# Two gates of the third branch among the mixers' last steps, two LoRA inputs projected later, and block values turned in written order

## The chip, the cores and the metric

The kernel runs on one core of a Trainium2 chip. The metric is the device time of one execution in microseconds (us), inputs and outputs in the chip's memory. A core has five engines that run side by side and are joined by semaphores: TensorE (PE) for matmuls, VectorE (DVE), ScalarE (ACT), GpSimd (POOL) and SyncE (SP), which here issues the DMA transfers of the weights.

## The reference

One layer of an encoder trunk, 256 positions, model width 2048, all in float32. After a norm, one projection feeds three branches: stick-breaking attention (4 heads of 128), forgetting attention (4 heads of 128) and an RWKV-7 time mixer (16 heads of 64), each weighted by a gate of its own:

```
u = rms_norm(x)
sb, fox, rw, gates = split(u @ w_in)
y_a = stick_breaking_attention(sb)
y_b = forgetting_attention(fox)            # with a forget logit per head
y_c = rwkv7_time_mix(rw)                   # r, k, v and LoRA inputs of decay, iclr and gate
g_a, g_b, g_c = split(sigmoid(gates))
m = g_a * (y_a @ P_a) + g_b * (y_b @ P_b) + g_c * (y_c @ P_c)
x = x + rms_norm(m @ w_out)
x = x + rms_norm(relu(rms_norm(x) @ w_up)**2 @ w_down)
```

Inside the time mixer each position is mixed with the one before it (a shift with weights mu), the decay comes from `tanh(wd) @ w_up`, the output gate from `sigmoid(gd) @ g_up`; a state per head runs through four chunks of 64 positions, and the output is normed per head.

## The kernel before

**Precision and weights.** Every large product is made of three float32r products: a value x is split into a high part (`hi`, a copy on ScalarE, L144) and a rest (`lo`, a subtraction on VectorE, L145), and hi*hi, hi*lo and lo*hi are summed in PSUM. All weights lie in one stream `wst` of tiles of 128 x 1024 (512 KB) in the order of use. `wraw` loads the next (L136, on SP's queue, three buffers `raw`), `wsplit` makes `whi` and `wlo` from it (three buffers each), and `wnext` keeps one split tile ahead. The stages are, in order: q and k of the first branch; its v; three LoRA inputs `zx` (decay and iclr), `zy` and `zz` (gate; `zz` also holds the forget logits); q, k, v of the second branch; k, r, v of RWKV heads 0 to 7 and then 8 to 15; gates and branch products of the first two branches; those of the third; W_out; the MLP.

**Two kinds of big product.** `unit` makes 128 features for all positions (L160, L164, L166; 16 tiles of `upk`, the split normed input). `tok` makes 512 features for the two halves of the positions (two PSUM tiles; L204, and L189 for its last tiles): for each pair of 128-row blocks of weights 8 matmuls with `whi` and 4 with `wlo`, all of 512 columns. `gate` is a `tok` over `upk` with a tanh into `th`; `branch` is a `tok` over a branch's split outputs (`ya`, `yb`, `ycp`), whose result is multiplied by the gate and added to the block's value `m` (L809 to L812). There are four blocks of 512 features.

**The mixers.** The recurrences and attentions themselves are small matmuls with much work on VectorE and ScalarE between. They are written as generators (`sb_mix`, `fox_mix`, `rwkv_lora`, `rwkv_half(0)` and `rwkv_half(1)`) that yield after each step. `tick` is called by `unit` and `tok` every few matmuls: it adds 0.62 of its argument to a credit and takes steps as long as there is credit. A yield `("stage", cost, hold)` also stops the steps until `hold` ticks have passed (2 by default). That is how small matmuls come to stand between big ones, on TensorE in the order in which they are written: `tc.manual_schedule` keeps TensorE to that order, while the other engines' order is chosen by the scheduler. `order.__exit__` ends this, and behind it the scheduler sets TensorE's order too.

**The steps of an RWKV half** that the prediction speaks of, with the lines of the profile: a triangular solve in 31 small steps on VectorE (L618, L620), transposes of its result (L624, L628), products of 32 x 32 blocks (L633, L640), and then for each of four chunks c: the right-hand side (L659 from c = 1, L663, copied to `rh` by L667), the solve (L672, copied to `Xt` by L676 and L678), and state and output (L683 from c = 1, L689, L692; the state `Pb` is updated by L698 and L700, the output copied by L702). Then the output norm for two pairs of heads each: squares L714, sums L718, gate products L721 and L724, rsqrt, and the products that finish `y` (L731 to L734), which becomes `yc[p]`.

**Where the third branch stands.** Behind the four blocks of the first two branches, a loop takes all steps that are left (`while not fin[0]: step()`), `order.__exit__` follows, the eight `yc` are split to `ycp`, and each block g does: gate, branch product, then four turns of the block's value: two transposes to PSUM (L835) and a split into `pk`, the operand of W_out. The pool `pk` has 24 buffers: 16 hold `upk` until the last gate, 8 hold `ycp`.

Of the kernel before, what the change touches and what calls it, by code (L numbers as in the profile page):

```python
# [49 lines left out]
def hybrid_block(ctx, tc, xt, x, gains, params, consts, lora, gup, wst, out):  # L50
# [47 lines left out]
    hold = [0.0]  # L98

    def step():  # L100

        if mix[0] is None or fin[0] or (wait[0] is not None and wait[0] not in done):
            return False
        wait[0] = None
        try:
            r = next(mix[0])
        except StopIteration:
            fin[0] = True
            return False
        if isinstance(r, tuple):  # L110
            if r[0] == "need":
                wait[0] = r[1]
                return True
            credit[0] -= r[1]
            if r[0] == "stage":
                hold[0] = r[2] if len(r) > 2 else 2.0
            return r[0] != "stage"
        credit[0] -= r
        return True

    def tick(f=1.0):

        credit[0] = min(credit[0] + f * SHARE, 1.5)
        hold[0] -= f
        while hold[0] <= 0 and credit[0] > 0 and step():
            pass


    wpos = [0]

    wq = []
    side = []

    def wraw(n=None):
        raw = wpool.tile([128, HALF], F32, tag="raw", name=nm("raw"), bufs=3)
        nc.sync.dma_start(out=raw, in_=wst[wpos[0] if n is None else n])  # L136
        if n is None:
            wpos[0] += 1
        return raw
# [232 lines left out]
    def fox_mix():  # L372
# [16 lines left out]
        V.tensor_tensor_scan(lf, one, m0, 0.0, ALU.mult, ALU.add)  # L389
        yield ("stage", 2.0, 6)  # L390
        ps = mps()
# [35 lines left out]
        for h in range(4):  # L427
            V.tensor_scalar(w[:, h, 0:128], w[:, h, 0:128], ri[:, h:h + 1], None, ALU.mult)
            V.tensor_scalar(w[:, h, 128:384], w[:, h, 128:384], ri[:, 4 + h:5 + h], None, ALU.mult)
            yield ("stage" if h == 3 else "go", 0.4, 4)  # L430
        for hp in range(2):
# [42 lines left out]
    def rwkv_half(hf):  # L474
# [160 lines left out]
        for g in range(4):  # L635
            A.activation(TW[32:64, g:32:4, :], ps[32 * g:32 * g + 32, 0:256].rearrange("p (a b) -> p a b", a=8), AF.Copy)
        yield ("stage", 0.2, 3)
        ps = mps()
# [3 lines left out]
        for g in range(4):  # L642
            A.activation(SC[0:32, g:32:4, 32:64], ps[32 * g:32 * g + 32, 0:256].rearrange("p (a b) -> p a b", a=8),
                         AF.Copy)
        yield ("stage", 0.2, 3)

# [5 lines left out]
        for c in range(4):  # L652
# [13 lines left out]
            for hc in HC:  # L666
                A.activation(rhs[:, :, hc], psr[hc, 0:T].rearrange("p (a b) -> p a b", a=4), AF.Copy)  # L667
            yield ("stage", 0.9)
            pso = [mps(), mps()]
# [3 lines left out]
            for i, p in enumerate(PR):  # L673
                for hc in HC:
                    if i < 2:
                        V.tensor_copy(Xt[p][0:64, c, hc], pso[0][hc, co[i]])  # L676
                    else:
                        A.activation(Xt[p][0:64, c, hc], pso[1][hc, co[i]], AF.Copy)  # L678
            yield ("stage", 0.9)
            psy = mps()  # L680
# [20 lines left out]
            for i, p in enumerate(PR):  # L701
                A.activation(y[p][:, c * 64:c * 64 + 64], psy[:, co[i]], AF.Copy)  # L702
            yield ("stage", 2.0)

        for i2 in range(2):
# [7 lines left out]
            for i in range(2):  # L713
                A.activation(sc[:, i, :], y[PR[2 * i2 + i]], AF.Square)  # L714
            yield ("stage", 0.1)
            ps = mps()
# [8 lines left out]
            A.activation(var, ps.rearrange("p (a b) -> p a b", a=2), AF.Identity, scale=1.0 / 64, bias=cst[:, 1:2])  # L725
            yield ("stage", 0.1)
            rsqrt(ri, var, sc)
# [31 lines left out]
    for br in ("sb", "fox"):  # L759
# [10 lines left out]
        done[br + "v"] = vtok()  # L770
        if br == "sb":
            done["sb"] = True
            for i, (nme, n) in enumerate((("zx", 128), ("zy", 128), ("zz", 36))):
                ps = unit(upk)
                z = rp.tile([64 if n == 36 else n, T], F32, name=nme)
                shift(ps, MU_X + i, z[0:n], n)
                done[nme] = z
            done["lora"] = True
        else:
            done["fox"] = True  # L780

# [13 lines left out]

    def gate():
        ths = []
        for ps in tok(upk):
            th = rp.tile([128, 512], F32, tag="th", name=nm("th"), bufs=3)
            A.activation(th, ps, AF.Tanh, scale=0.5)  # L800
# [14 lines left out]
    for g in range(4):  # L815
        m = rp.tile([128, 2, 512], F32, tag="m", name=nm("m"), bufs=4)
        branch(ya, gate(), m, True)
        branch(yb, gate(), m, False)
        ms.append(m)
    while not fin[0]:  # L820
        step()
    order.__exit__(None, None, None)
    ycp = []
    for p in range(8):
        y = pk()
        split(yc[p], y)
        ycp.append(y)
    mpk = []
    for g in range(4):
        thc = gate()  # L830
        branch(ycp, thc, ms[g], False)
        for j in range(4):
            ps = mps()
            for tt in range(2):
                PE.transpose(ps[:, tt * 128:tt * 128 + 128], ms[g][:, tt, j * 128:j * 128 + 128], C("ident"))  # L835
            u = pk()
            split(ps[:, 0:T], u, 0.5)
            mpk.append(u)
    p1.close()
# [24 lines left out]

    g2, loads = gain(0, [fm().rearrange("p a b -> p (a b)")[:, 0:512] for _ in range(4)])
    x1 = [p2.tile([128, D], F32, tag="x1", name=nm("x1"), bufs=2) for _ in range(2)]
# [15 lines left out]
    for g in range(4):  # L882
        gs = slice(512 * g, 512 * g + 512)
        for tt, ps in enumerate(tok(mpk, 4 if g == 3 else 1)):
            def gained():
# [418 lines left out]
```

## Time and profile before

| what | us |
|---|---|
| median of 3 runs | 1560.79 |
| lowest, highest | 1556.21, 1565.39 |
| the profiled execution | 1562.27 |
| its span from first to last instruction | 1560.5 |
| steps of RWKV half 0 up to its first output norm | 361.83 to 440.02 |
| the same steps of half 1, and its second output norm | 592.37 to 643.08 |
| from there to the second set of turns | 643.08 to 667.98 |

A line of the profile names the source line, the engine, what is written and read, the shape, and how many instructions; a line of the timeline begins with start and length in us, and a bracket at its end tells how long the engine was idle before it and who released it. Matmuls are pipelined: one of 512 columns is listed at about 0.39 us, but the next starts earlier, so lengths overlap and starts are what counts. In a table by stretch the columns are the stretch, its length, busy time and number of instructions of TensorE, the mean granted clock (1.00 is full speed), the busy share of the DMA engines, and GB/s.

### The profile page before, as it was taken

How to read it: one execution, taken by the hardware profiler on the slowest of the kernel's cores; microseconds unless marked ns; L12 is line 12 of the kernel's file. 1: busy time of each engine (PE TensorE's matmuls, PEld its weight loads, DVE VectorE, ACT ScalarE, POOL GpSimd, SP SyncE). 2: the span in 40 equal slices, each digit the busy share in tenths (PEclk: the TensorE clock that was granted, in tenths of full speed). 3: DMA queues.
4: the chain of work that ended last, by engine and by line, in shares of the span. 5: the costliest groups of instructions: out<-in, count | busy, mean ns of one | idle time of the engine just before them, and what ended most of it. 6: DMA issues, size and time to landing. Idle time of an engine off the chain costs nothing.

```text
span 1560.5 us, 22381 instructions
## 1 busy us (share of the span) xinstructions
PE 1524.2 (98%) x8318; PEld 1265.7 (81%) x8318; DVE 1157.1 (74%) x1566; ACT 907.9 (58%) x1369; POOL 88.5 (6%) x146
## 2 busy tenths in 40 slices
PE   7999999999999999999999999999999999999997
PEld 6888887887887787788887888888888877888885
DVE  7765568896558896645555778789988899888855
ACT  7565367545466554644444766567766676666542
POOL 0030001100001100000000000000000000000000
PEclk9999999999999998999999999999999999999999
DMA  7645554455445553355695557798888888887764
GB/s 242 206 159 176 162 165 150 138 190 189 135 144 179 174 164 96 125 180 188 228 306 164 171 188 201 216 266 254 242 257 250 230 236 239 263 253 232 214 200 136
DMA packets 101197, 308.50 MB, mean 198 GB/s; under 512 B 10080, under 2 KB 12512, under 8 KB 101088
## 3 DMA queue, kind: packets, MB, share of 16 engines
q1 hardware_dynamic: 91344, 280.66, 55.1%
q0 software_dynamic: 6912, 25.17, 8.7%
q8 instruction: 65, 1.06, 0.3%
q10 hardware_dynamic: 2832, 1.24, 0.3%
q14 instruction: 44, 0.36, 0.1%
HBM read 279.77 MB, written 2.10 MB: 181 GB/s over the span
## 4 chain that ended last, share of the span: by engine, by line
PE 66%; issue 10%; DVE 10%; DMA 9%; ACT 4%; POOL 0%; ACTq 0%; SPq 0%; POOLq 0%; DVEq 0%
PE gps L204 27%; PE gps L160 15%; PE gps L164 8%; DMA raw<-raw 5%; PE gps L189 5%; DVE wlo L145 5%; DMA raw<-in_wst_dram 4%; ACT whi L144 2%; PE gps L166 1%; PE mps L1069 1%; PE mps L1071 1%; PE mps L1070 1%; PE gps L1071 1%; PE gps L1069 1%; PE gps L1070 1%
## 5 line engine op out<-in xcount | busy, mean ns | idle before, releaser
L145 DVE TENSOR_TENSOR wlo<-raw,whi 128x1024 fp32r<-128x1024 f32 x590 | 716.1, 1223 | 272.4 <-ACT whi L144 254.4
L144 ACT ACTIVATE whi<-raw 128x1024 fp32r<-128x1024 f32 x590 | 618.2, 1055 | 342.0 <-PE gps L204 153.8
L160 PE MATMUL gps<-pk,whi 128*128 128x512 f32 x1501 | 386.2, 395 | 2.1 <-ACT whi L144 1.0
L160 PEld LDWEIGHTS gps<-pk,whi 128*128 128x128 f32 x1501 | 278.2, 189 | 62.4 <-issue 5.8
L204 PE MATMUL gps<-whi,pk 128*128 128x512 f32 x1144 | 293.8, 395 | 0.4 <-ACT whi L144 0.4
L204 PEld LDWEIGHTS gps<-whi,pk 128*128 128x128 f32 x1144 | 213.5, 189 | 47.0 <-issue 1.3
L164 PEld LDWEIGHTS gps<-pk,wlo 128*128 128x128 f32 x1608 | 220.1, 191 | 16.0 <-DVE wlo L145 0.7
L164 PE MATMUL gps<-pk,wlo 128*128 128x256 f32 x1608 | 225.9, 283 | 0.1
L204 PE MATMUL gps<-wlo,pk 128*128 128x512 f32 x572 | 159.8, 397 | 0.4 <-DVE wlo L145 0.4
L204 PEld LDWEIGHTS gps<-wlo,pk 128*128 128x128 f32 x572 | 107.3, 190 | 24.2 <-DVE wlo L145 1.1
L991 ACT ACTIVATE tmp<-gps 128x256 f32<-128x256 f32 x64 | 24.6, 384 | 90.7 <-PE gps L166 90.7
L1069 PE MATMUL mps<-whi,fm 128*128 128x512 f32 x192 | 76.1, 396 | 0.8 <-ACT whi L144 0.7
L1071 PE MATMUL mps<-wlo,fm 128*128 128x512 f32 x192 | 75.5, 393 | 0.4 <-DVE wlo L145 0.2
L1070 PE MATMUL mps<-whi,fm 128*128 128x512 f32 x192 | 75.0, 391 | 0.0
L1036 POOL DMA_DIRECT2D raw<-raw x48 | 41.9, 873 | 554.2 <-DVE raw L1033 313.2
L189 PE MATMUL gps<-whi,pk 128*128 128x512 f32 x264 | 71.3, 393 | 0.0
L1071 PE MATMUL gps<-wlo,fm 128*128 128x512 f32 x144 | 57.2, 397 | 2.4 <-DVE wlo L145 2.1
L1033 DVE TENSOR_TENSOR raw<-raw,raw 128x1024 f32<-128x1024 f32 x48 | 58.7, 1223 | 1.0
L189 PEld LDWEIGHTS gps<-whi,pk 128*128 128x128 f32 x264 | 49.2, 188 | 11.2 <-issue 0.7
L1069 PE MATMUL gps<-whi,fm 128*128 128x512 f32 x144 | 56.8, 395 | 1.4 <-ACT whi L144 1.4
L1070 PE MATMUL gps<-whi,fm 128*128 128x512 f32 x144 | 56.5, 392 | 0.0
L204 PE MATMUL gps<-whi,fm 128*128 128x512 f32 x208 | 51.4, 389 | 0.0
(294 smaller groups left out, 1551.7 us busy)
## 6 DMA issues: line engine op xcount, KB each, us to landing
raw<-in_wst_dram SPq DMA_DIRECT2D x518, 512.0 KB, 4.4
raw<-raw POOLq DMA_DIRECT2D x48, 512.0 KB, 6.7
x<-in_x_dram SPq DMA_DIRECT2D x8, 256.0 KB, 6.5
out_dram<-x SPq DMA_DIRECT2D x8, 256.0 KB, 2.8
x<-in_xt_dram SPq DMA_DIRECT2D x3, 512.0 KB, 7.3
fm<-in_gains_dram SPq DMA_DIRECT2D x4, 256.0 KB, 5.5
pk<-in_gains_dram SPq DMA_DIRECT2D x4, 256.0 KB, 4.5
con<-in_consts_dram SPq DMA_DIRECT2D x1, 576.0 KB, 7.8
```

The lines of the kernel that those rows point to most:

```text
L144: A.activation(hi, raw, AF.Copy)
L145: V.tensor_tensor(lo, raw, hi.bitcast(F32), ALU.subtract)
L160: PE.matmul(ps, hi[:, i * 128:i * 128 + 128], pks[i], start=first and i == 0, stop=False)
L164: PE.matmul(ps[:, 0:T], lo[:, i * 128:i * 128 + 128], pks[i][:, 0:T], start=False, stop=False)
L189: PE.matmul(ps[tt], pks[k][:, c:c + 128], w[:, (k - k0) * 512:(k - k0) * 512 + 512], start=k == 0 and part == 0 and w is hl[0], stop=w is ...
L204: PE.matmul(ps[tt], pks[k][:, c:c + 128], w[:, (k - k0) * 512:(k - k0) * 512 + 512], start=k == 0 and part == 0 and w is hl[0], stop=False)
L991: A.activation(b, ps[0][:, T:2 * T], AF.Copy)
L1033: V.tensor_tensor(R[a], R[a], R[b], ALU.add)
L1036: G.dma_start(out=R[a], in_=R[b], accum_op=ALU.add)
L1069: PE.matmul(Q[f], a, w, start=d == 0 and i == 0, stop=False)
L1070: PE.matmul(Q[f], b, w, start=False, stop=False)
L1071: PE.matmul(Q[f], a, wl, start=False, stop=d == 3 and i == 1)
```

## The change

It has five parts, and leaves the arithmetic as it was.

1. The first two gates of the third branch are made before the loop that takes the remaining steps, so under the written order and with ticks (`thc`; the second one's tanh goes to free buffers of the pool `BK`). Weights are still in their old places in the stream, so `wraw` follows a small table of jumps.
2. `order.__exit__` moves behind the third block of W_out: the third branch and most of W_out keep the written order. The turns become hooks: one is taken at each tick, those of blocks 0 to 2 from the 13th tick of the last block's gate on, those of the last block from the fifth tick of W_out on.
3. `yc[p]` is split as soon as it is there, at any tick (`cut`).
4. `zx` and `zy` are projected behind the second branch; `zz` stays where it was.
5. Holds of several steps are shorter (6 to 4, 4 to 3, 3 to 2, 2 to 1, 2 to 1.7), and one has no hold. The gains of the norm behind W_out are loaded at once, and no longer one for each weight tile.

```diff
+    each, hooks = [], []
...
         while hold[0] <= 0 and credit[0] > 0 and step():
             pass
+        for f in each:
+            f()
+        if hooks:
+            hooks.pop(0)()
...
+    gc = wst.shape[0] - 256 - 32 - 48
+    jump = {23: 28, 53: 24, 27: 54, gc + 7: gc + 12, gc + 19: gc + 8, gc + 11: gc + 20}
...
-            wpos[0] += 1
+            wpos[0] = jump.get(wpos[0], wpos[0] + 1)
...
-        yield ("stage", 2.0, 6)
+        yield ("stage", 2.0, 4)
...
-            yield ("stage" if h == 3 else "go", 0.4, 4)
+            yield ("stage" if h == 3 else "go", 0.4, 3)
...
-        yield ("stage", 0.2, 3)
+        yield ("stage", 0.2, 2)
...
-            yield ("stage", 0.9)
+            yield ("stage", 0.9, 1)
...
-            yield ("stage", 2.0)
+            yield ("stage", 1.5, 1.7)
...
-            yield ("stage", 0.1)
+            yield ("stage", 0.1, 1)
...
-            yield ("stage", 0.1)
+            yield ("stage", 0.1, 0)
...
-        if br == "sb":
-            done["sb"] = True
-            for i, (nme, n) in enumerate((("zx", 128), ("zy", 128), ("zz", 36))):
...
+        done[br] = True
+        for i, nme, n in ((0, "zx", 128), (1, "zy", 128)) if br == "fox" else ((2, "zz", 36),):
+            ps = unit(upk)
...
+    ycp = [None] * 8
+
+    def cut():
+        for p in range(8):
+            if yc[p] is not None and ycp[p] is None:
+                ycp[p] = pk()
+                split(yc[p], ycp[p])
+
+    cut()
+    each.append(cut)
+    thc = [gate(), gate("BK", 8)]
     while not fin[0]:
         step()
-    order.__exit__(None, None, None)
...
+    cut()
+    each.clear()
+    mpk = [None] * KT
+
+    def turn(g, j):
+        ps = mps()
+        for tt in range(2):
+            PE.transpose(ps[:, tt * 128:tt * 128 + 128], ms[g][:, tt, j * 128:j * 128 + 128], C("ident"))
+        mpk[4 * g + j] = pk()
+        split(ps[:, 0:T], mpk[4 * g + j], 0.5)
+
     for g in range(4):
-        thc = gate()
-        branch(ycp, thc, ms[g], False)
...
+        if g == 3:
+            hooks.extend([lambda: None] * 12 + [lambda k=k: turn(k // 4, k % 4) for k in range(12)])
+        branch(ycp, thc.pop(0) if thc else gate(), ms[g], False)
+    hooks.extend([lambda: None] * 4 + [lambda j=j: turn(3, j) for j in range(4)])
+    wo = tok(mpk)
+    lead = [next(wo)]
...
-    g2, loads = gain(0, [fm().rearrange("p a b -> p (a b)")[:, 0:512] for _ in range(4)])
+    g2, now = gain(0, [fm().rearrange("p a b -> p (a b)")[:, 0:512] for _ in range(4)])
+    for f in now:
+        f()
+    loads = []
...
-        for tt, ps in enumerate(tok(mpk, 4 if g == 3 else 1)):
+        if g == 3:
+            order.__exit__(None, None, None)
+        for tt, ps in enumerate(itertools.chain(lead, wo) if g == 0 else tok(mpk, 4 if g == 3 else 1)):
```

Lines move by 10 to 12 in the new file: L633 is L643 there, L640 is L650, L663 is L673, L672 is L682, L683 is L693, L724 is L734, L835 is L847, and of the big matmuls L189 and L204 are L199 and L214. The order of instructions on an engine is shown at two places; a row is an instruction, what it writes and reads, its size, and a count.

TensorE before, at the first block products of RWKV half 1 (`SC` and `TW` are its solved blocks, `gps_6078` and `gps_6079` the two PSUM tiles of the third branch's first gate):

```order
L633 MATMUL mps_5664<-TW_5660,SC_4702 32x32 x32
L204 MATMUL gps_6078<-whi_5624,pk_281 128x512 x2
L204 MATMUL gps_6079<-whi_5624,pk_281 128x512
L640 MATMUL mps_5701<-SC_4702,TW_5660 32x32 x2
L204 MATMUL gps_6079<-whi_5624,pk_281 128x512
L204 MATMUL gps_6078<-whi_5624,pk_286 128x512
L640 MATMUL mps_5701<-SC_4702,TW_5660 32x32
L204 MATMUL gps_6078<-whi_5624,pk_286 128x512
L640 MATMUL mps_5701<-SC_4702,TW_5660 32x32 x29
L663 MATMUL mps_5744<-Xt_5287,SC_4702 64x64 x2
```

and TensorE of the change at the same products (`gps_5472` and `gps_5473` belong to the last gate of the second branch here):

```order
L643 MATMUL mps_5510<-TW_5406,SC_4413 32x32 x32
L214 MATMUL gps_5472<-whi_5494,pk_401 128x512 x2
L214 MATMUL gps_5473<-whi_5494,pk_401 128x512 x2
L214 MATMUL gps_5472<-whi_5494,pk_406 128x512 x2
L214 MATMUL gps_5473<-whi_5494,pk_406 128x512 x2
L214 MATMUL gps_5472<-wlo_5495,pk_401 128x512
L214 MATMUL gps_5473<-wlo_5495,pk_401 128x512
L214 MATMUL gps_5472<-wlo_5495,pk_406 128x512
L214 MATMUL gps_5473<-wlo_5495,pk_406 128x512
L214 MATMUL gps_5472<-whi_5549,pk_461 128x512 x2
L214 MATMUL gps_5473<-whi_5549,pk_461 128x512 x2
L650 MATMUL mps_5575<-SC_4413,TW_5406 32x32 x32
```

Before, three big matmuls stand ahead of the second product and single ones in its midst; now sixteen stand between the two products, and the second one is whole. Counted in weight pairs of the stream, the first product stands at the 182nd pair before and at the 174th now; on VectorE the last of the transposes L628 (L638 now) stands behind the 183rd weight split before and behind the 169th now.

TensorE before, at the first turns of a block's value (`m_3359`; `gps_6330` and `gps_6331` belong to the next gate):

```order
L204 MATMUL gps_6330<-whi_6286,pk_281 128x512 x2
L204 MATMUL gps_6331<-whi_6286,pk_281 128x512
L835 MATMUL mps_6306<-ident,m_3359 128x128
L835 MATMUL mps_6312<-ident,m_3359 128x128
L835 MATMUL mps_6318<-ident,m_3359 128x128
L835 MATMUL mps_6324<-ident,m_3359 128x128
L204 MATMUL gps_6331<-whi_6286,pk_281 128x512
```

and TensorE of the change at its first turns, in the last block's gate:

```order
L214 MATMUL gps_6762<-whi_6819,pk_521 128x512 x2
L847 MATMUL mps_6845<-ident,m_3384 128x128 x2
L214 MATMUL gps_6761<-whi_6819,pk_526 128x512 x2
L214 MATMUL gps_6762<-whi_6819,pk_526 128x512 x2
L214 MATMUL gps_6761<-wlo_6820,pk_521 128x512
L214 MATMUL gps_6762<-wlo_6820,pk_521 128x512
L847 MATMUL mps_6857<-ident,m_3384 128x128 x2
```

Before, the first turns stand right behind the block's third-branch product; now they stand three blocks later, both transposes of a turn side by side, with two to six big matmuls between turns.

More of the change, by code (lines that the diff above doesn't have):

```diff
@@ L1 @@
+import itertools
 import math
@@ L644, in rwkv_half @@
                          AF.Copy)
-        yield ("stage", 0.2, 3)
+        yield ("stage", 0.2, 2)
         Pb = rp.tile([128, 4, 128], F32, tag="Pb", name=nm("Pb"), bufs=1)
@@ L678, in rwkv_half @@
                         A.activation(Xt[p][0:64, c, hc], pso[1][hc, co[i]], AF.Copy)
-            yield ("stage", 0.9)
+            yield ("stage", 0.9, 1)
             psy = mps()
@@ L770, in hybrid_block @@
         done[br + "v"] = vtok()
-        if br == "sb":
-            done["sb"] = True
-            for i, (nme, n) in enumerate((("zx", 128), ("zy", 128), ("zz", 36))):
[L774 to L780, printed above, removed]
+        done[br] = True
+        for i, nme, n in ((0, "zx", 128), (1, "zy", 128)) if br == "fox" else ((2, "zz", 36),):
+            ps = unit(upk)
+            z = rp.tile([64 if n == 36 else n, T], F32, name=nme)
+            shift(ps, MU_X + i, z[0:n], n)
+            done[nme] = z
+    done["lora"] = True
     for hf in range(2):
@@ L794, in hybrid_block, with gate @@
     ya, yb = done["ya"], done["yb"]
-    def gate():
+    def gate(tag="th", bufs=3):
         ths = []
         for ps in tok(upk):
-            th = rp.tile([128, 512], F32, tag="th", name=nm("th"), bufs=3)
+            th = rp.tile([128, 512], F32, tag=tag, name=nm("th"), bufs=bufs)
             A.activation(th, ps, AF.Tanh, scale=0.5)
@@ L819, in hybrid_block @@
         ms.append(m)
+    ycp = [None] * 8
[7 more added lines that the diff above has]
+    thc = [gate(), gate("BK", 8)]
     while not fin[0]:
         step()
-    order.__exit__(None, None, None)
[L823 to L828, printed above, removed]
-    for g in range(4):
-        thc = gate()
-        branch(ycp, thc, ms[g], False)
[L832 to L838, printed above, removed]
+    cut()
[7 more added lines that the diff above has]
+        split(ps[:, 0:T], mpk[4 * g + j], 0.5)
+    for g in range(4):
+        if g == 3:
[4 more added lines that the diff above has]
+    lead = [next(wo)]
     p1.close()
```

## The prediction

> **What bounds the kernel now.** I read the page's busy shares first, then the waits of TensorE, then tables by stretch for the stages that the change touches, and last the timeline around each wait.
>
> ```profile
> PE 1524.2 (98%) x8318; PEld 1265.7 (81%) x8318; DVE 1157.1 (74%) x1566; ACT 907.9 (58%) x1369; POOL 88.5 (6%) x146
> PE   7999999999999999999999999999999999999997
> PEclk9999999999999998999999999999999999999999
> ```
>
> TensorE is busy 98% of the span, and the change neither adds nor removes a matmul. So time can only come from three places: waits of TensorE, stretches at a lower clock, and switches that make matmuls slower than their steady pitch. That pitch:
>
> ```profile
> 433.95 1.98 PE L204 MATMUL gps<-whi,pk 128*128 128x512 f32 x8
> 435.76 1.07 PE L204 MATMUL gps<-wlo,pk 128*128 128x512 f32 x4
> 436.67 1.07 PE L204 MATMUL gps<-whi,pk 128*128 128x512 f32 x4
> ```
>
> Twelve matmuls of 512 columns ("big" below; one pair of weight tiles) start between 433.95 and 436.67: 2.72 us, so 0.2267 us each. With this a stage can be weighed. Half 0 of the RWKV steps (from its L633 to the end of its first output norm, L724) runs among big matmuls under the written order. Half 1 does the same in the drain loop, with little beside it. The first three rows below are all of TensorE in half 0, in half 1 and in the stretch behind half 1; the next three are the same windows with big matmuls alone.
>
> ```profile
> 361.83:440.02 78.19, 78.19 (x709) 1.00 0.50 159
> 592.37:643.08 50.71, 47.91 (x545) 0.90 0.30 95
> 643.08:667.98 24.90, 22.44 (x95) 0.93 0.43 135
> 361.83:440.02 78.19, 62.41 (x257) 1.00 0.50 159
> 592.37:643.08 50.71, 25.71 (x81) 0.90 0.30 95
> 643.08:667.98 24.90, 21.52 (x85) 0.93 0.43 135
> ```
>
> Half 0: 78.19 - 257 x 0.2267 = 19.9 us for its small matmuls. Half 1: 50.71 - 81 x 0.2267 = 32.3 us. Its window holds one output norm more (640.52 to 643.08, 2.6 us), so 29.8 us stand against 19.9: **9.9 us too many**. The third stretch: 24.90 - 85 x 0.2267 = 5.6 us for eight turning matmuls (some 0.1 us each), **4.8 us too many**. Together 14.7 us, and the views say what they are:
>
> ```profile
> PE mps L835 <- DVE m L812: 2.1, 1, 2.1
> PE mps L640 <- DVE SC L628: 2.0, 1, 2.0
> PE mps L718 <- ACT gn L714: 0.8, 1, 0.8
> ...
> 593.05 0.97 PE L204 MATMUL gps<-whi,pk 128*128 128x512 f32 x3
> 594.00 1.90 DVE L628 STREAM_TRANSPOSE SC<-Ti 32x1024 f32<-32x1024 f32 x1
> 596.04 0.25 PE L640 MATMUL mps<-SC,TW 32*32 32x32 f32 x4 [2.02 <-DVE SC L628]
> ...
> 598.00:608.00 10.00, 10.00 (x98) 0.50 0.49 159
> ```
>
> Three waits make 4.9 us (columns: total, times, longest). The clock column is a mean, and in half 1 it is 0.90: 10% of 50.71 us, 5.1 us, is lost to a stretch at half clock, which begins within 2 us of the wait for L628; 0.93 of 24.90 us loses 1.7 us more behind the wait for L812. That is 11.7 of 14.7 us. The rest is cutting: L640 and L659 are split by single big matmuls here, and each split costs.
>
> **The change, part by part.** *Two gates under the written order.* Two gates of the third branch are two times eight pairs of weight tiles: 16 x 2.72 = 43.5 us of big matmuls, which no step of half 1 has to wait for. Which engine is late there: L628 turns the solved triangles on VectorE, L640 reads them. Before, the last L628 stands behind the 183rd weight split of VectorE and L640 at the 183rd weight pair of TensorE, so nothing lies between. Now they stand at the 169th and the 176th (L638 and L650 in the new file). VectorE works in order and TensorE cannot pass the 169th pair before the next split, which is behind the transposes: six pairs, 16 us, cover a wait of 2.0. Its half-clock stretch should go with it, and the steps stand whole as in half 0. Term: -9.9 us. Behind the last step TensorE has 68 big matmuls left before the first that reads yc, and 36 more before the one that reads its last pair: 23.6 us, against the 9.4 us of the norm's chain (below) and four products and splits of some 0.4 us behind it. No wait there.
>
> *Turning in written order.* Turns of the first three blocks start twelve ticks into the last gate, those of the last block four ticks into W_out's first block, when block values have long been added. The wait for L812 and its half clock go: -4.8 us. But 32 transposes come in 16 visits where there were 11. Two visits of four in a calm stretch:
>
> ```profile
> 755.00:775.00 20.00, 19.99 (x93) 1.00 0.68 214
> 755.00:775.00 20.00, 19.41 (x85) 1.00 0.68 214
> ```
>
> 85 records (two cut by the window's ends) x 0.2267 and eight transposes leave 0 to 0.4 us, so 0 to 0.2 us a visit; 5 more visits are 0 to 1 us, and if every visit paid the 0.36 us that a split pays, 1.8 us. I take 0.9.
>
> *Shorter holds.* Steps of the recurrence now follow after one tick, in both halves. What each needs when its engines are free is seen in half 1, where nothing else was in the way:
>
> ```profile
> 616.27 0.68 PE L663 MATMUL mps<-Xt,SC 64*64 64x64 f32 x16
> 617.06 0.78 ACT L667 ACTIVATE rh<-mps 64x256 f32<-64x256 f32 x2 [2.52 <-PE mps L663]
> 617.79 0.78 PE L672 MATMUL mps<-rh,SC 64*64 64x64 f32 x16
> 618.38 0.98 DVE L676 COPY Xt<-mps 64x64 f32<-64x64 f32 x4 [1.81 <-PE mps L672]
> 618.61 0.95 ACT L678 ACTIVATE Xt<-mps 64x64 f32<-64x64 f32 x4 [0.77 <-PE mps L672]
> 619.54 0.69 PE L689 MATMUL mps<-Xt,Kt 128*64 128x64 f32 x16
> 620.05 0.64 PE L692 MATMUL mps<-SC,Xt 128*64 128x64 f32 x16
> 620.29 0.88 DVE L698 TENSOR_TENSOR Pb<-mps,Pb 64x256 f32<-64x256 f32 x2 [0.94 <-PE mps L689]
> 621.20 0.87 DVE L700 TENSOR_TENSOR Pb<-Pb,ecol 64x256 f32<-64x256 f32 x2
> 621.75 0.33 PE L659 MATMUL mps<-Pb,Bt 128*64 128x64 f32 x2
> ...
> L145 DVE TENSOR_TENSOR wlo<-raw,whi 128x1024 fp32r<-128x1024 f32 x590 | 716.1, 1223 | 272.4 <-ACT whi L144 254.4
> L144 ACT ACTIVATE whi<-raw 128x1024 fp32r<-128x1024 f32 x590 | 618.2, 1055 | 342.0 <-PE gps L204 153.8
> ```
>
> L663 to L672 takes 1.5 us from start to start, 0.9 behind the end of L663; L672 to L689 is 1.75 us, 1.05 behind its end; L689 to L659 is 2.2 us. The order now leaves at the least 6 big matmuls for the first (1.36 us), 6 to 8 and mostly L683 besides for the second (1.36 to 2.8 us), 12 and L692 for the third (3.4 us). All fit. A weight split of 1.06 us on ScalarE ahead of L667 would make 0.6 us of wait, one of 1.22 us on VectorE ahead of L676 0.9 us where L683 is not between, two ahead of Pb 0.8 us. On ScalarE the order sets a split behind each pair of steps rather than between, so I take 0; the bound is eight first steps x 0.6, two second ones x 0.9 and six third ones x 0.8: 11.4 us over both halves. Below nothing: TensorE was not waiting in half 0 (clock 1.00, no row of waits), so an earlier half 0 gains nothing.
>
> *Second output norm.* It waits for the buffer of the first:
>
> ```profile
> 631.11 0.70 PE L724 MATMUL mps<-zz,gup 32*128 32x256 f32 x4
> 640.07 0.71 ACT L714 ACTIVATE gn<-g 128x256 f32<-128x256 f32 x2
> 640.52 1.13 PE L718 MATMUL mps<-gn,con 128*128 128x256 f32 x4 [0.78 <-ACT gn L714]
> ```
>
> The chain takes 9.4 us; the order now leaves 48 big matmuls, 10.9 us, but two tanh of 0.6 us come in on ScalarE. So the 0.8 us wait may stay or go; the 9.9 us count it as gone, so I add +0.8 to be fair, of 0 to 1.5.
>
> *Inputs of decay and gate later.* Three projections, shifts and their activations change places; TensorE's count, the number of table loads (23) and SP's 543 transfers stay. The stream's jumps are other addresses for the same 512 KB tiles. Three memsets of 0.1 us move on POOL, which is idle. Their first user comes some 300 rows later on TensorE. Term 0. In that stretch the clock drops once, without any wait:
>
> ```profile
> 182.31 1.97 PE L401 MATMUL mps<-foxf,ident 4*128 4x256 f32 x8
> 184.00:190.00 6.00, 6.00 (x26) 0.72 0.22 79
> ```
>
> 0.28 x 6 is 1.7 us; it may fall elsewhere or vanish: -1.7 to +1.7, taken as 0.
>
> *Gain loads at once, splits of yc per tick.* SP issues the gains two weight tiles later, where they wait for the last turn, and weights queue behind them.
>
> ```profile
> raw<-in_wst_dram SPq DMA_DIRECT2D x518, 512.0 KB, 4.4
> ```
>
> The first weight behind them is read 60 big matmuls (13.6 us) after that turn; landing and both splits take 4.4 + 1.06 + 1.22 = 6.7 us. Covered; if not, a wait of the difference, none here. Eight splits of yc are the same instructions, earlier. Term 0.
>
> **Sum.** -9.9 - 4.8 + 0.9 + 0.8 = -13.0 us. The profiled execution took 1562.3 us (span 1560.5), so it would take 1549.3; the median of the runs shown, 1560.8, lies 1.5 lower, so I predict **1547.8 us**.
>
> **The rivals.**
> *The half clock stays (chance 0.07).* It may follow from many small matmuls, not from the waits: at 184 us it fell without a wait. Against it: half 0 has the same small matmuls at 1.00. If both stretches stay, 5.1 + 1.7 us come back: 1554.6. [...]
> *Shorter holds become waits (0.14).* ScalarE and VectorE hold a weight split ahead of a step more often than the order of before suggests. Two thirds of the bound, 7.6 us, comes back: 1555.4. For it: 1.36 us of cover against 0.9 + 1.06. Against: the engines' order.
> *Waits that gate the clock: slower (0.04).* The place is L663 to L672 in both halves. If each step waits as bounded (11.4 us) and the waits, which come every 10 us or so, each bring a half-clock stretch like the one of 1.7 us, eight of these add 13.6 us: 1547.8 + 25 = 1572.8. It decides from about 13 us given back, so from where waits begin to gate; the wait of 0.78 us before L718 did not (598 to 608 alone makes up the mean of 0.90).
> *It does not do what it says:* steps left for a drain behind the gates. The order shows L734, the last step, inside the second gate, so I give this no chance of its own.
>
> **How the numbers follow.** Forecast 0.75, rivals 0.07, 0.14, 0.04. A measurement tells about 0.5% (7.8 us, so 1553 and 1568.6) from no change. The forecast is faster, and a fifth of the second rival's cases too: 0.78. The other cases of the first two are within: 0.18; slower 0.04. The range of eight in ten: low -14.7 - 1.7 and some 3 us of scatter between runs, 1541; high takes in both middle rivals, 1557.
>
> **What would show it.** Right: no row of waits for L640 (now L650) or for L835 (L847); half 1's small matmuls cost about 20 us as half 0's; the granted clock is 1.00 from half 1 to W_out. Wrong: rows that wait for rh, Xt or Pb in both halves; a clock below 0.95 in half 1; a wait before the first matmul that reads the last yc; or whi and wlo as the releasers of big matmuls there.

## The result and the profile after

| | before | changed kernel |
|---|---|---|
| median of 7 runs, us | 1562.17 | 1547.59 |
| lowest, highest | 1556.21, 1565.39 | 1542.72, 1551.39 |
| the profiled execution | 1562.27 | 1549.40 |
| its span | 1560.5 | 1547.6 |

The ratio is 0.9906, with a 95% interval from 0.9885 to 0.9927: 14.6 us faster by the medians, 12.9 by the profiled executions. The page's busy shares and the row of the clock:

```profile
PE 1515.7 (98%) x8318; PEld 1262.7 (82%) x8318; DVE 1155.4 (75%) x1566; ACT 908.4 (59%) x1369; POOL 92.9 (6%) x146
PEclk9999999999999999999999999999999999999998
```

The number of matmuls is the same, and TensorE's share is 98% as before, so the share says nothing about the gain. The waits of TensorE do (columns: total, times, longest); these are all of 0.3 us and more:

```profile
PE gps L170 <- ACT whi L154: 9.0, 2, 8.4
PE mps L931 <- DVE x L900: 2.1, 2, 1.9
PE gps L1095 <- DVE wlo L155: 1.5, 4, 0.6
PE gps L1093 <- ACT whi L154: 1.4, 1, 1.4
PE mps L1095 <- DVE wlo L155: 1.0, 3, 0.5
PE gps L199 <- DVE wlo L155: 0.9, 1, 0.9
PE gps L170 <- DVE tmp L1016: 0.8, 3, 0.3
PE gps L174 <- DVE wlo L155: 0.8, 1, 0.8
PE mps L931 <- DVE pk L236: 0.7, 1, 0.7
PE mps L1093 <- ACT whi L154: 0.7, 1, 0.7
PE gps L214 <- DVE wlo L155: 0.3, 1, 0.3
PE mps L650 <- ACT TW L646: 0.3, 2, 0.2
```

The three rows of before that carried 4.9 us (L640 for the solve, L835 for a block's value, L718 for the second output norm) have no successor: L650 now waits 0.3 us, and for ScalarE; L847 and L728 have no row. Next, half 1 in a table by stretch, from its first product L643 to the end of its second output norm: all of TensorE, then big matmuls alone.

```profile
571.45:644.03 72.58, 72.58 (x685) 1.00 0.42 139
571.45:644.03 72.58, 54.51 (x221) 1.00 0.42 139
```

72.58 - 221 x 0.2267 = 22.5 us for small matmuls. Without the second norm (641.58 to 644.03, 2.45 us) that is 20.0 us, where 29.8 stood before and half 0 had 19.9. The clock is 1.00.

**One stretch for all kernels.** To compare kernels whose steps stand in different places, I count big matmuls in TensorE's order. From the 2400th to the 3200th lie, in each kernel below, all of half 1 from L643 on and all 32 turning matmuls, and nothing else besides the 800 big ones; 1297 records of TensorE each time (one straddles the edge). Its length is "the stretch" from here on. Before, then after:

```profile
563.26:786.66 223.40, 218.13 (x1297) 0.97 0.53 169
```

```profile
564.10:772.00 207.90, 207.90 (x1297) 1.00 0.55 181
```

The stretch is 15.5 us shorter. The 1000 big matmuls ahead of it, which hold half 0, went the other way by 1.6 us, the rest of the program by 1.0: -15.5 + 1.6 + 1.0 = -12.9, the difference of the two profiled executions.

### The profile page after: what moved, and what is told of

Same layout as the page of the kernel before. It is cut to its first block, busy times and chain, and to the rows that moved or that the text cites. A ratio compares the mean times of both kernels' runs of the same rounds, so it can differ in the third digit from the quotient of the medians.

```text
span 1547.6 us, 22370 instructions
## 1 busy us (share of the span) xinstructions
PE 1515.7 (98%) x8318; PEld 1262.7 (82%) x8318; DVE 1155.4 (75%) x1566; ACT 908.4 (59%) x1369; POOL 92.9 (6%) x146
## 4 chain that ended last, share of the span: by engine, by line
PE 74%; DVE 9%; issue 8%; DMA 6%; ACT 2%; POOL 0%; SPq 0%; DVEq 0%; POOLq 0%; ACTq 0%
PE gps L214 29%; PE gps L170 15%; PE gps L174 9%; PE gps L199 7%; DVE wlo L155 4%; DMA raw<-raw 4%; DMA raw<-in_wst_dram 3%; PE mps L1093 1%; PE mps L1095 1%; ACT whi L154 1%; PE mps L1094 1%; PE gps L1095 1%; PE gps L176 1%; PE gps L1093 1%; PE gps L1094 1%
## 5 line engine op out<-in xcount | busy, mean ns | idle before, releaser
L214 PE MATMUL gps<-whi,pk 128*128 128x512 f32 x1144 | 291.7, 394 | 0.0
L214 PEld LDWEIGHTS gps<-whi,pk 128*128 128x128 f32 x1144 | 212.0, 188 | 46.0 <-issue 2.3
L214 PE MATMUL gps<-wlo,pk 128*128 128x512 f32 x572 | 155.3, 391 | 0.3 <-DVE wlo L155 0.3
L214 PEld LDWEIGHTS gps<-wlo,pk 128*128 128x128 f32 x572 | 106.8, 188 | 23.0 <-DVE wlo L155 0.8
L199 PE MATMUL gps<-whi,pk 128*128 128x512 f32 x264 | 72.0, 395 | 0.0
L199 PEld LDWEIGHTS gps<-whi,pk 128*128 128x128 f32 x264 | 48.7, 188 | 10.8 <-issue 0.5
L214 PE MATMUL gps<-whi,fm 128*128 128x512 f32 x208 | 51.4, 389 | 0.0
```

Of the source, the lines that this page charges most:

```text
L199: PE.matmul(ps[tt], pks[k][:, c:c + 128], w[:, (k - k0) * 512:(k - k0) * 512 + 512], start=k == 0 and part == 0 and w is hl[0], stop=w is ...
L214: PE.matmul(ps[tt], pks[k][:, c:c + 128], w[:, (k - k0) * 512:(k - k0) * 512 + 512], start=k == 0 and part == 0 and w is hl[0], stop=False)
```

## The experiments

Each kernel was timed in five rounds beside the kernel before on the same chip, except the probe. "The drain" is the loop that takes the steps which are left. Line numbers are those of each kernel's own file; they differ from the changed kernel's by a few. In the edits, `...` stands for lines left out, and the table of jumps, which follows the places of gates and inputs, is adapted in each kernel and mostly not shown. Most single removals come first, then parts alone, then a probe of the clock. The table puts the results together. Its second column is half 1's first product, its third the place of the drain (both in big matmuls of TensorE's order), and the stretch is that of one profiled execution each. The medians come from four sets of rounds, in which the kernel before took 1560.9 to 1562.2 us; the ratios compare within a set.

| kernel | half 1 from | drain at | stretch, us | median, us | ratio, 95% interval |
|---|---|---|---|---|---|
| before | 2529 | 2529 | 223.4 | | 1 |
| gates alone | 2613 | 2721 | 221.7 | 1558.93 | 0.9987 (0.9972 to 1.0003) |
| holds, second mixer and half 0 | 2485 | 2529 | 216.5 | 1554.73 | 0.9961 (0.9945 to 0.9977) |
| holds alone | 2485 | 2529 | 214.6 | 1553.28 | 0.9953 (0.9937 to 0.9970) |
| holds and inputs | 2433 | 2529 | 212.4 | 1551.63 | 0.9937 (0.9915 to 0.9959) |
| gates and holds | 2485 | 2721 | 214.2 | 1553.81 | 0.9947 (0.9926 to 0.9969) |
| changed | 2433 | 2721 | 207.9 | 1547.59 | 0.9906 (0.9885 to 0.9927) |
| changed, old turns | 2433 | 2721 | 208.9 | 1547.20 | 0.9911 (0.9892 to 0.9931) |
| changed, old inputs | 2485 | 2721 | 209.6 | 1546.72 | 0.9910 (0.9893 to 0.9927) |
| changed, one gate | 2433 | 2625 | 219.1 | 1555.76 | 0.9969 (0.9947 to 0.9992) |
| changed, gates undone | 2433 | 2529 | 224.7 | 1562.88 | 1.0016 (1.0002 to 1.0030) |
| changed, old holds | 2565 | 2721 | 224.9 | 1560.97 | 1.0003 (0.9991 to 1.0015) |
| four gates, old holds, old turns | 2565 | 2913 | 211.6 | 1547.61 | 0.9931 (0.9904 to 0.9958) |

### The gates undone

```diff
-    thc = [gate(), gate("BK", 8)]
+    thc = []
```

and the table of jumps without the gates' entries.

> The changed kernel with the two gates of the third branch back behind the drain; everything else of the change stays. Theory (the gates' big matmuls cover half 1's steps): the stretch from half 1's first step to the end of its norms is 10.9 us shorter in the changed kernel than in the one before at the same work, and this comes back nearly whole: 8 to 12 us, so 1556 to 1560 us; a row of waits for L650 on the triangle transposes of about 2 us, and a clock below 0.95 in half 1. Rival (shorter holds and an earlier start of half 1 make the gain, the gates only stand nearby): under 3 us come back, so below 1551, and no wait for L650.

1562.88 us, 15.3 above the changed kernel's median. Waits of TensorE:

```profile
PE mps L728 <- ACT gn L724: 7.9, 2, 6.9
PE mps L669 <- DVE Pb L710: 1.5, 1, 1.5
PE mps L682 <- ACT rh L677: 0.5, 1, 0.5
PE mps L650 <- ACT TW L646: 0.2, 1, 0.2
```

The stretch:

```profile
563.84:788.49 224.65, 214.51 (x1297) 0.95 0.49 167
```

The loss is larger than expected and sits elsewhere: not at L650, since half 1 starts early enough for its solve, but in the last steps and norms. Since the order is written out up to W_out here, the drain stands bare: nothing lies between its steps, and each chain is waited for in full, the norm's with 6.9 us. In the kernel before, the scheduler put big matmuls of the first gate between them, one to four at a time, and 34 between the two norms. So this removal also shows what part 2 does to a drain, and not the gates alone. The clock is 0.50 from 611.56 to 632.03 us, right through that drain.

### Turning as before

```diff
-        if g == 3:
-            hooks.extend([lambda: None] * 12 + [lambda k=k: turn(k // 4, k % 4) for k in range(12)])
         branch(ycp, thc.pop(0) if thc else gate(), ms[g], False)
-    hooks.extend([lambda: None] * 4 + [lambda j=j: turn(3, j) for j in range(4)])
+        for j in range(4):
+            turn(g, j)
```

with the order released behind the drain.

> The changed kernel with the merged blocks turned behind each gate and product, outside the written order, as before; the two gates stay ahead. Theory (TensorE waits for the last addition of a block because the turns follow it at once): a wait of about 2 us for the first turn and a half-clock stretch behind it come back, 4.6 us in all, so 1552 us (1551 to 1554). Rival (that wait came from the drain, whose late yc made the first block late): with the gates ahead there is no wait for L847 either way, and under 1.5 us come back.

1547.20 us, and this theory falls: no wait for the turns, the clock 1.00, and a stretch 1.0 us longer than the changed kernel's.

```profile
563.63:772.52 208.89, 208.88 (x1297) 1.00 0.53 181
```

### The old holds

```diff
-            yield ("stage", 0.9, 1)
+            yield ("stage", 0.9)
...
-            yield ("stage", 1.5, 1.7)
+            yield ("stage", 2.0)
```

and the others as in the diff of the change, all in reverse.

> The changed kernel with the longer holds of before between the steps, in both halves. Theory (the shorter holds cost the 1.6 us that half 0 lost, and half 1 has room for the longer ones inside the two gates): half 0 gets 1 to 1.6 us back, the row of waits for L650 on ScalarE goes, and half 1 stays: 1546 to 1548 us. Rival (without the shorter holds half 1's last steps fall behind the gates): the last steps stand in a drain again and lose 2 to 5 us there, so 1549 to 1552.

1560.97 us: the whole gain is gone, and both expectations were far too small. Half 1 starts at the 2565th big matmul instead of the 2433rd, only its first two rounds fit ahead of the drain at 2721, and the rest stands bare as above:

```profile
PE mps L728 <- ACT gn L724: 7.9, 2, 6.9
PE mps L669 <- DVE Pb L710: 1.2, 1, 1.2
```

### The inputs where they were

```diff
-        for i, nme, n in ((0, "zx", 128), (1, "zy", 128)) if br == "fox" else ((2, "zz", 36),):
+        for i, nme, n in ((0, "zx", 128), (1, "zy", 128), (2, "zz", 36)) if br == "sb" else ():
```

> The changed kernel with the inputs of decay and gate projected where they were before. Theory (their place is worth nothing to TensorE): within 1 us of the changed kernel, 1547 to 1548.5; the one half-clock stretch near 170 us may move. Rival (the later place delays the mixers' early steps, or half 1 starts early only because of it): half 1's steps move by several weight pairs and 2 us or more are lost or won.

1546.72 us, as the theory has it, although half 1 starts 52 big matmuls later: all of it still ends ahead of the drain. The stretch is 1.7 us longer, which the medians don't show.

### Two parts alone: gates and holds

The kernel before with parts 1, 3 and the holds of part 5; behind the drain it goes on as before.

```diff
+    cut()
+    each.append(cut)
+    thc = [gate(), gate("BK", 8)]
     while not fin[0]:
         step()
+    cut()
+    each.clear()
     order.__exit__(None, None, None)
```

> The kernel before with two parts of the change alone: the two gates (with the splits of yc per tick) and the shorter holds. Turning, the inputs of decay and gate, and the gain loads stay as before. Theory (the whole gain is that no step of half 1 is left to the drain, which takes both parts together): the full gain, 1546 to 1549 us, no wait for L640's or L835's successors, clock 1.00 from half 1 to W_out. Rival (the written turns or the other parts carry some of it, hidden in the single removals): 1550 to 1554.

1553.81 us: half of the gain, inside the rival's range. One wait is back, for the first turn (L848 here):

```profile
PE mps L848 <- DVE m L819: 2.1, 1, 2.1
```

```profile
562.49:776.70 214.21, 211.27 (x1297) 0.99 0.53 179
```

So the wait ahead of the first turn is no part of half 1. Two kernels differ from this one in little, and neither has it: with the inputs later (and the gains at once) it is "changed, old turns", 5.3 us shorter in the stretch; with turns in written order (and the gains at once) it is "changed, old inputs", 4.6 us shorter. In the first, half 1's last norm stands 54 big matmuls earlier, and VectorE is through with it when the first block is finished; in the second nobody reads the block at once. Either cover is enough, which is why removing one of the two cost next to nothing.

### Cover instead of short holds: four gates

The old holds and old turns, with all four gates of the third branch ahead of the drain.

```diff
-    thc = [gate(), gate("BK", 8)]
+    thc = [gate(), gate("BK", 8), gate("BK", 8), gate("BK", 8)]
```

> The changed kernel with the longer holds of before, all four gates of the third branch ahead of the drain, and the turning as before. By the engines' order half 1's last output norm then stands inside the fourth gate. Theory (the gain follows from cover alone; shorter holds only make the steps fit into two gates): the 13 us that the longer holds cost with two gates come back with four: 1546 to 1549 us, half clock gone between 560 and 770 us. Rival (the shorter holds themselves are the gain): 1557 to 1562, as with the longer holds and two gates.

1547.61 us, 13.4 below two gates with the same holds. The wait for the first turn, 1.5 us, is in this kernel too, and accounts for part of the stretch of 211.6.

```profile
561.70:773.27 211.57, 209.31 (x1297) 1.00 0.53 179
```

Its runs scatter from 1543.9 to 1557.3, so its interval is the widest. The order is also released behind the drain here, but no step is left in it. Short holds are not needed if the cover is long enough, and the last step stands ahead of the drain.

### Shorter holds alone

The kernel before with the holds of part 5, all as in the diff of the change:

```diff
-            yield ("stage", 0.9)
+            yield ("stage", 0.9, 1)
...
-            yield ("stage", 2.0)
+            yield ("stage", 1.5, 1.7)
```

> The kernel before with the shorter holds alone. Theory (holds without cover only let half 1 start a little earlier; its last steps still share the drain, where the scheduler mixes single big matmuls in): 1558 to 1562 us, half-clock stretches in half 1 stay. Rival (the holds are the gain): below 1553.

1553.28 us. My theory falls: holds alone bring 7.6 us. Half 1 starts 44 big matmuls ahead of the drain, so its solve ends under the written order, the wait of L640 is gone, and no half clock follows. The rest of the drain's waits stay:

```profile
PE mps L835 <- DVE m L812: 1.5, 1, 1.5
PE mps L718 <- ACT gn L714: 0.8, 1, 0.8
```

```profile
562.52:777.14 214.62, 212.07 (x1297) 1.00 0.52 178
```

### Gates alone

"Gates and holds" with all holds as before, among them:

```diff
-            yield ("stage", 1.5, 1.7)
+            yield ("stage", 2.0)
```

> The kernel before with the two gates (and the splits of yc per tick) alone, longer holds as before. In the order half 1 then starts 84 big matmuls later than in the kernel before (2613 against 2529) but under the written order, and 3 of its 4 rounds still share the drain with the third branch's work. Theory A (the price of half 1 before is the solve's end in the drain, a wait for L628 and the half clock behind it, and either gates or shorter holds take it out of the drain): 1552 to 1555 us, no wait for L640, as with shorter holds alone (1553.3). Theory B (shorter holds are needed whatever the cover): 1559 to 1562 us.

1558.93 us, 2.6 below the kernel before, at the edge of theory B and no difference that the interval is sure of. The wait of L640 is gone as theory A says, but a new one stands in its place:

```profile
PE gps L199 <- ACT pk L232: 5.1, 1, 5.1
```

```profile
561.66:783.33 221.67, 213.61 (x1297) 0.98 0.49 171
```

L199 is the third branch's first product, L232 the split of the last `yc`. With its gate already made, nothing is left between the end of half 1 and its reader. Two gates ahead only move the wait if the steps don't fit into them.

### Shorter holds ahead of half 1 alone

The kernel before with the shorter holds in the second branch's mixer and, in `rwkv_half`, by the half:

```diff
-            yield ("stage", 0.9)
+            yield ("stage", 0.9, 1 if hf == 0 else 2.0)
...
-            yield ("stage", 2.0)
+            yield ("stage", 1.5, 1.7) if hf == 0 else ("stage", 2.0)
```

> The kernel before with the shorter holds in the second branch's mixer and in half 0 alone; half 1 keeps the longer ones. Half 1's solve then ends under the written order as with all holds shorter, but its four rounds start in the drain. Theory (a head start for half 1 is what shorter holds bring): 1552 to 1556 us, no wait for L640 and its half clock. Rival (denser steps in half 1 are what they bring): 1558 to 1562 us.

1554.73 us, as the theory has it: a head start for half 1 brings 6.8 of the 7.6 us that all holds bring. Its own denser steps add 1.9 us of the stretch (216.47 against 214.62), which the two intervals don't tell apart.

### Holds and inputs

"Holds alone" with part 4:

```diff
+    jump = {23: 28, 53: 24, 27: 54}
...
+        for i, nme, n in ((0, "zx", 128), (1, "zy", 128)) if br == "fox" else ((2, "zz", 36),):
```

> The kernel before with the shorter holds and the later inputs, without gates or written turns. Half 1 starts at big matmul 2433 instead of 2485 with the holds alone, and only its last round and a half and its norms are left to the drain. Theory (what the drain costs is the work left to it): 1549 to 1553 us, between the holds alone (1553.3) and the changed kernel (1547.6). Rival (the inputs' place is worth nothing, as its single removal said): 1553 to 1554.

1551.63 us, as the theory has it: the inputs' later place is worth 2.3 us of the stretch where a drain is left (212.36 against 214.62), and nothing where none is. The intervals of the two ratios overlap, so this rests on the stretch.

### One gate instead of two

```diff
-    thc = [gate(), gate("BK", 8)]
+    thc = [gate()]
```

> The changed kernel with one gate ahead of the drain instead of two. By the order all steps of half 1 but the last output norm stand inside it; that one stands 20 big matmuls (4.5 us) behind the first, which takes 9.4 us. Theory (an uncovered chain is waited for at its full length): a wait for L728 of about 5 us and perhaps one half-clock stretch of 3.4 us, so 5 to 7 us over the changed kernel: 1552 to 1555 us. Rival (the first gate's big matmuls bridge it): under 2 us, 1547 to 1549.

1555.76 us, somewhat above the expected range.

```profile
PE gps L199 <- ACT pk L232: 3.8, 1, 3.8
PE mps L728 <- ACT gn L724: 3.4, 1, 3.4
```

The norm waits 3.4 us, not 5, and the third branch's first product 3.8 us, which I had not seen. The mean clock of the stretch is 0.98, which two half-clock stretches of 3.41 us would make in 219.1 us. With one behind each of the two waits, 1.7 us lost in each, that is an estimate of 10.6 of the 11.2 us by which this stretch is longer than the changed kernel's.

### What lowers the clock

```diff
+        PE.transpose(ps[:, 0:128], C("ident"), C("ident"))
+        V.tensor_copy(held[:, 0:128], ps[:, 0:128])
+        for _ in range(n):
+            V.tensor_scalar(held, held, 1.0, None, ALU.mult)
+        PE.transpose(ps[:, 0:128], held[:, 0:128], C("ident"))
```

ahead of blocks 1, 2 and 3 of the third branch, with n = 1, 3 and 7.

> The changed kernel with three waits put into the third branch, where TensorE runs big matmuls alone: a transpose, a chain of VectorE operations of growing length on it, and a transpose of its result, so that TensorE waits some 1, 2 to 3 and 4 to 6 us with no small matmuls near. It tells what brings the half clock. Theory of the prediction (waits of 2 us bring it): half clock behind the second and third, not the first. Rival (many small matmuls bring it): none behind any of them. [...]

In the one execution of this kernel the waits came out at 1.90, 3.74 and 5.59 us, somewhat longer than planned:

```profile
672.19 0.30 PE L861 MATMUL mps<-ident,held 128*128 128x128 f32 x1 [1.90 <-DVE held L859]
688.88 0.33 PE L861 MATMUL mps<-ident,held 128*128 128x128 f32 x1 [3.74 <-DVE held L859]
727.59 0.48 PE L861 MATMUL mps<-ident,held 128*128 128x128 f32 x1 [5.59 <-DVE held L859]
```

Between the first and the last matmul, the half-clock stretches are 3.41, 10.24, 3.41 and 3.41 us long in the kernel before, 3.41 and 6.82 us in the changed kernel, and 20.47 us in the drain of "gates undone": 3.41 us or a multiple of it. In the kernel before they begin at 185.04, 598.05, 662.90 and 857.46 us, which is 121, 19 and 57 of these lengths apart (10.24 / 3 us each). So I cut the time around the waits into slices of that length, in step with the half-clock stretches:

```profile
669.95:673.37 3.42, 1.52 (x9) 1.00 0.42 149
673.37:676.78 3.41, 3.41 (x10) 0.50 0.41 154
676.78:680.19 3.41, 3.41 (x16) 1.00 0.30 119
683.61:687.02 3.41, 1.53 (x8) 1.00 0.42 161
687.02:690.43 3.41, 1.55 (x7) 1.00 0.41 135
690.43:693.85 3.42, 3.42 (x16) 1.00 0.07 24
721.15:724.57 3.42, 0.86 (x5) 1.00 0.42 155
724.57:727.98 3.41, 0.39 (x2) 0.50 0.46 154
727.98:731.39 3.41, 3.41 (x10) 0.50 0.00 0
731.39:734.80 3.41, 3.41 (x17) 1.00 0.00 0
```

The wait of 1.90 us lies within one slice, leaves it 1.52 us of work, and the next slice has a clock of 0.50. The wait of 3.74 us is cut in two by a slice's edge, leaves 1.53 and 1.55 us in the two slices, and the clock stays 1.00. Both expectations fall: the length of a wait alone didn't decide. Nor do these rows show a limit for the work in a slice: 1.52 us and 1.53 us lie on different sides. The waits for the first turn, cut in step with the half-clock stretches of their own traces, left 1.36 us in the kernel before, with 0.50 behind it, and 1.88 us in four gates, with 1.00. Here first the kernel before, then four gates:

```profile
659.48:662.90 3.42, 1.36 (x9) 1.00 0.85 292
662.90:666.31 3.41, 3.41 (x12) 0.50 0.54 171
```

```profile
711.94:715.36 3.42, 1.88 (x10) 1.00 0.70 224
715.36:718.77 3.41, 3.41 (x20) 1.00 0.69 235
```

So a wait of some 2 us was followed by half clock, an estimated 1.7 us more (half of 3.41), in some kernels and not in others. Of the six kernels with this wait, two have half clock behind it (before, gates and holds; 2.1 us each), and four have not (holds alone, holds first, holds and inputs, four gates; 1.3 to 2.0 us, the mean clock of the stretch 1.00). Differences of that size between two stretches of one execution each can be chance.

Busy time alone didn't decide either. In the kernel before, the slice in which the wait for L628 ends has 2.00 us of work, 64 of its 67 matmuls small ones of L640, and the next has a clock of 0.50; in the changed kernel a slice that TensorE filled, 12 of its 18 matmuls with only 4 rows of weights, was followed by 0.50 without any wait:

```profile
594.63:598.04 3.41, 2.00 (x67) 1.00 0.49 154
598.05:601.45 3.40, 3.40 (x37) 0.50 0.48 159
```

```profile
167.19:170.60 3.41, 3.41 (x18) 1.00 0.31 91
170.60:174.01 3.41, 3.41 (x13) 0.50 0.37 133
```

## Why the prediction was right, point by point

*The sum.* -13.0 us was forecast, 1547.8; 1547.59 was measured. What was to go, 14.7 us in half 1 and behind it, did go: 15.5 us in the stretch. Half 1's small matmuls cost 20.0 us where "as half 0's" said 19.9, the rows for L640 and L835 are gone, and the clock is 1.00. The size of the loss was read rightly. Which part of the change removes it was not. That the time agrees to 0.2 us is luck: the 0.9 and 0.8 us that were added for turns and norm didn't come, 1.6 us ahead of the stretch and 1.0 us elsewhere came in their place, and seven runs put the kernel before 1.4 us higher than the three runs that the forecast started from.

*Two gates under the written order: -9.9.* Wrong as a price of the gates. Alone they take 1.7 us off the stretch; holds alone take 8.8. The positions that I quoted (L640 from the 183rd weight pair to the 176th) are the work of the holds and the inputs, not of the gates: with gates alone half 1 starts later, at 2613 for 2529. What gates do is to move the drain from 2529 to 2721. Under the written order of part 2 that is needed: without the gates or without the short holds the drain stands bare, and the gain is gone (+1.3 and +1.5 us of the stretch against before). But these two removals price the bare drain and not the parts. Where the order is released at the drain, the scheduler fills it, and the two gates add 1.7 us to nothing else, 0.4 to the holds (214.6 to 214.2, where the wait for the first turn and its half clock come back: 2.1 us, and 0.99 for the stretch) and 3.5 to holds and inputs (212.4 to 208.9, "changed, old turns", with the gains at once). Holds and inputs without gates already have 11.0 of the 15.5 us, with the last steps still in the drain. So most of the gain is the shorter holds and the earlier start.

*Shorter holds: 0, "so an earlier half 0 gains nothing."* This is the step that failed. I asked whether TensorE waits in half 0, and it doesn't; but half 1 follows half 0, so a shorter half 0 is a head start for half 1, and this head start, with the shorter holds of the second branch's mixer, is worth 6.8 us by itself. The feared waits came out at 0.3 us, all at L650 of half 0:

```profile
350.46 0.24 PE L650 MATMUL mps<-SC,TW 32*32 32x32 f32 x2 [0.16 <-ACT TW L646]
350.86 0.70 PE L650 MATMUL mps<-SC,TW 32*32 32x32 f32 x58 [0.16 <-ACT TW L646]
```

They and the slow products around them (1.74 us from the first L650 to the next big matmul, 0.68 from L640 in half 0 before) are the larger part of the 1.6 us that the stretch of half 0 lost, against a bound of 11.4.

*Turning in written order: -4.8, and +0.9 for more visits.* The term is about right where half 1 ends late (4.6 us between "gates and holds" and "changed, old inputs", of which some 1.7 are the half clock that only two of the six kernels with such a wait show), and 1.0 us where it ends early. In the changed kernel both covers are there, so the wait can't be put down to one of them. The 0.9 was too cautious: more visits showed no cost that the comparison could tell.

*Second output norm: +0.8.* The wait went. With nothing beside its chain it cost 6.9 us (gates undone), with 20 big matmuls between 3.4 us (one gate), so the 48 between were needed.

*Inputs later: 0.* Right as a single removal, wrong as a rule: 2.3 us with the holds alone, through the earlier start of half 1. "Their first user comes some 300 rows later" looked at who waits for the moved work and not at what moves up into the freed place. (SP's 543 transfers are 549 in both traces; the argument needs only that they are equal.)

*The clock.* "Its half-clock stretch should go with it" was right in the result: 0.97 to 1.00. That waits of 2 us bring it is not shown: in the probe 3.41 us at 0.50 followed the wait of 1.90 us, and none the wait of 3.74 us; of the six waits for the first turn, of 1.3 to 2.1 us, two had half clock behind them.

*The rivals.* Neither the remaining half clock nor waits from shorter holds came in any size, and nothing like the slower case.

*What stays open.* What brings the half clock. With big matmuls and a few transposes, a slice with 1.52 us of work was followed by 0.50 and one with 1.53 us by 1.00 in the probe; 2.00 us with many small matmuls and 3.41 us with some of 4 rows were followed by 0.50 as well. And the 1.0 us outside the two stretches is a sum of -0.7 ahead of them, +0.9 where the residual is turned (L931; the clock is 0.50 from 843.03 to 849.85 us, where it was 0.50 for half as long before, from 857.46 to 860.87), and +0.9 in the MLP; no run tested these.

None of the other versions beats the changed kernel by more than the intervals allow: old turns, old inputs and four gates all lie within 1 us of it by their medians.

## What to carry to other kernels

Work without dependants is worth little as cover if the chain that it is to cover doesn't end inside it, and no more than that chain's waits and splits if it does; ask of every step that is moved or sped up what starts earlier behind it, also where nobody waits. Parts of a change that act on one wait, each enough by itself, show nothing when they are removed one by one, and a part that keeps another part's cost away shows more than it brings: removing the gates cost 16.8 us of the stretch, adding them brought 0.4 to 3.5. Price parts by adding as well as by removing. A chain left bare at the end of a written order cost its full length here (a wait of 6.9 us for the second norm with the gates undone), and half clock on top (0.50 for 20.47 us).

## What the runs showed of the hardware

Between the first and the last matmul, the half-clock stretches lasted 3.41 us or a multiple of it: 3.41 to 10.24 us in the kernel before, 3.41 and 6.82 us in the changed kernel, 20.47 us in the bare drain with the gates undone. In the probe a wait of 1.90 us was followed by 3.41 us at 0.50, an estimated 1.7 us lost, while behind a wait of 3.74 us the clock stayed 1.00. In the changed kernel half clock also followed a slice of 3.41 us that TensorE filled with work (167.19 to 170.60 us), so neither waits nor busy time alone decided.
